# Low halves of the token mixers' projection weights by a negated copy and an adding transfer

## The chip, the cores and the metric

The kernel runs on one core of a Trainium2 chip. The metric is the device time of one execution in microseconds (us). The engines are named as in the profile: PE is TensorE (PEld its weight loads), ACT ScalarE, DVE VectorE, POOL GpSimd, SP SyncE; SP and POOL issue the transfers (DMAs). A time difference of about 0.2% (2.5 us) is what a measurement of this kernel can tell from no change.

## The reference

The trunk of an encoder with 512 tokens of width 1024, in float32, in two layers. Cut to what matters here:

```
x, mem                                  # 512 x 1024, 256 x 1024
layer A: h = rmsnorm(x)
  proj = h @ a_w_in                     # 1024 x 3336: q,k (conv, silu) | v | o | gates | q_mem
  mix  = mlstm(q, k, v, gates) * sigmoid(o)
  x += concat(mix, memory_attention(q_mem, mem)) @ a_w_out
  x += conv_ffn(rmsnorm(x))             # ffn_w_up 1024 x 5632, ffn_w_down 2816 x 1024
k, v = rmsnorm(x) @ w_kv                # 1024 x 1536, shared
layer B: h = rmsnorm(x)
  q, q_mem = h @ b_w_in                 # 1024 x 1024
  x += concat(band_attention(q, k, v), memory_attention(q_mem, mem)) @ b_w_out
  x += conv_ffn(rmsnorm(x))
return rmsnorm(x)
```

## The kernel before, in words

Every large product is made of three matmuls in the type float32r, which holds fewer bits than float32. A float32 operand a is written as two halves: the high one is a rounded to float32r, the low one is a minus the high one. The product is then high times high, high times low and low times high, added up in PSUM (`mm3`, L161 to L164; the low half of the weights is read in L164). Activations are split when they are made. Weights are split as they arrive: SP loads a tile of 128 x 1024 floats (512 KB) into one of three raw buffers `wr` (`load`, L135), ACT casts it to the high half `wh` (L129), and DVE subtracts that from the raw tile and writes the low half `wl` (L130); `parts` and `weights` (L147 to L155) are these two steps. `wh` and `wl` have three buffers each too, so a tile can be prepared once the tile three places earlier has been used up.

`project` (L166) takes eight row blocks of 128 of one column block of weights as a tile and makes 24 matmuls of 128x512 with it. It is called by `qk_tile` (12 tiles), `o_tile` (6) and `a_memory_queries` (2) on `a_w_in`, by `project_pair` (12 tiles of `w_kv`, 6 of `b_w_in`) and `b_memory_queries` (2) in layer B, and by `OutProjection.finish` and `ffn_hidden`, which take other weights. I number the twenty tiles of layer A that `project` loads as A1 to A20 and the twenty of layer B as B1 to B20, in the order in which they are used. A1 follows the value columns of `a_w_in` (`value_columns`, whose tiles have 384 columns and are split in the old way before and after the change); B1 follows the last eight tiles of layer A's `ffn_w_down`.

Projections are the filler between the steps of the mixers: `weave` (L193) takes so many steps of the filler for each step of the attention job. The program is written with a tile framework whose scheduler sets the order on each engine from costs of its own, save for what is pinned, so a change in one place can move instructions elsewhere. Each engine then works its own list strictly in order. POOL's list holds transfers (`xspill` L898 and L956, `rep` L932 and L934, the bias rows of the band attention L1004) and small memsets (L480 for the query heads, L631 for the convolution).

Of the kernel before, what the change touches and what calls it, by code (L numbers as in the profile page):

```python
# [10 lines left out]
F32R = mybir.dt.float32r  # L11
I32 = mybir.dt.int32
AF = mybir.ActivationFunctionType
ALU = mybir.AluOpType
AX = mybir.AxisListType

P = 128
D = 1024
# [9 lines left out]
DFF = 2816  # L28
# [13 lines left out]
def f(ap):  # L42
    return ap.bitcast(F32)
# [3 lines left out]
def trunk(  # L47
# [19 lines left out]
    V, A, G = nc.vector, nc.scalar, nc.gpsimd  # L67
# [10 lines left out]
    def sb(tag, shape, dtype=F32):  # L78
        count[0] += 1
        return pool.tile(shape, dtype, tag=tag, name=f"{tag}{count[0]}", bufs=bufs[tag])  # L80

    def ps(tag):
        count[0] += 1
        return psum.tile([P, S], F32, tag=tag, name=f"p{tag}{count[0]}", bufs=pbufs[tag])
# [43 lines left out]
    def split(hi, lo, src, on_act=True, pinned=False):  # L128
        high = A.copy(hi, src) if on_act else V.tensor_copy(hi, src)  # L129
        low = V.tensor_tensor(out=lo, in0=src, in1=f(hi), op=ALU.subtract)  # L130
        if pinned:
            pin(high)
            pin(low)

    def load(src, a, b, extra=None):  # L135
        n = b + (extra.shape[-1] if extra is not None else 0)
        raw = sb("wr", [P, D])[:, : a * n].rearrange("p (a b) -> p a b", a=a)
        if isinstance(src, list):
            for i, one in enumerate(src):
                nc.sync.dma_start(raw[:, i, :], one)  # L140
        else:
            nc.sync.dma_start(raw[:, :, :b], src)
        if extra is not None:
            nc.sync.dma_start(raw[:, :, b:], extra)
        return raw

    def parts(raw, pinned=False):  # L147
        _, a, b = raw.shape
        hi = sb("wh", [P, D], F32R)[:, : a * b].rearrange("p (a b) -> p a b", a=a)
        lo = sb("wl", [P, D], F32R)[:, : a * b].rearrange("p (a b) -> p a b", a=a)  # L150
        split(hi, lo, raw, pinned=pinned)
        return hi, lo

    def weights(*args):
        return parts(load(*args))  # L155

    def rows(w, c0, n, k0=0, k1=None):
        k1 = k1 if k1 is not None else w.shape[0] // P
        return w[k0 * P : k1 * P, c0 : c0 + n].rearrange("(k p) c -> p k c", p=P)

    def mm3(o, lh, ll, rh, rl, first, last):  # L161
        nc.tensor.matmul(o, lh, rh, start=first, stop=False)  # L162
        nc.tensor.matmul(o, lh, rl, start=False, stop=False)  # L163
        nc.tensor.matmul(o, ll, rh, start=False, stop=last)  # L164

    def project(w, c0, act, tag="mm"):  # L166


        n = len(act)
        wh, wl = weights(rows(w, c0, P), n, P)  # L170
        o = ps(tag)
        for k in range(n):
            mm3(o, wh[:, k, :], wl[:, k, :], act[k][0], act[k][1], k == 0, k == n - 1)
            yield
        return o

    def run(gen):
        while True:
            try:
                next(gen)  # L180
            except StopIteration as end:
                return end.value
# [5 lines left out]
    def pair_of(a, b):  # L188
        first = yield from a
        second = yield from b  # L190
        return first, second

    def weave(job, filler, each, lead=0):  # L193

        due = lead
        for n in chain([0], job):
            due += each if n is None else each * n
            while due >= 1:
                due -= 1
                next(filler, None)  # L200
# [39 lines left out]
    class Norm:  # L240
# [14 lines left out]
        def finish(self):  # L255

            yield 5.4
            o = ps("sc")
            for T in range(TT):
                tc.keep_in_program_order(  # L260
                    nc.tensor.matmul(
                        o[:, T : T + 1], self.acc[:, T * P : (T + 1) * P], ones[:, 0:1], start=True, stop=True
                    )
                )
            self.factor(o[:, :TT])
            yield 8.4
            self.spread()
# [19 lines left out]
    def scaled(t, g):  # L287
        hi, lo = sb("u", [P, S], F32R), sb("u", [P, S], F32R)
        A.activation(hi, t, AF.Copy, scale=g)
        V.scalar_tensor_tensor(lo, t, g, f(hi), op0=ALU.mult, op1=ALU.subtract)  # L290
        return hi, lo
# [117 lines left out]
    with tc.manual_schedule(engines={mybir.EngineType.PE, mybir.EngineType.Activation, mybir.EngineType.DVE}):  # L409

        w = ps("mm")
# [7 lines left out]
        for q in range(KT // 2 + 1):  # L419
            if q < KT // 2:  # L420
# [6 lines left out]
                hi, lo = sb("u", [P, S], F32R), sb("u", [P, S], F32R)  # L427
# [160 lines left out]
    class OutProjection:  # L588
# [19 lines left out]
        def finish(self, gnames):  # L608
            norm = Norm()
            acts = [[] for _ in gnames]  # L610
            for j in range(KT):
                o = self.o[j] if j in self.o else run(project(self.w, j * P, self.mixes))
                V.tensor_add(xT[j], xT[j], o)
                norm.add(xT[j])
                for a, g in zip(acts, gnames):
                    a.append(scaled(xT[j], g[:, j : j + 1]))
            return norm, acts

    def ffn_hidden(l, j, act, norm):
        w = ffn_w_up[l]  # L620
        fw, fb = col[f"fw{l}"], col[f"fb{l}"]
        gate, up = project(w, DFF + j * P, act), project(w, j * P, act, "sc")
        og = ou = None
        if norm.row is None:
            both = pair_of(gate, up)
            weave(norm.finish(), both, 1)
            og, ou = run(both)
        else:
            og = run(gate)
        pre = sb("t", [P, S + 4])  # L630
        G.memset(pre[:, 0:2], 0.0)  # L631
        V.tensor_tensor(out=pre[:, 2 : S + 2], in0=og, in1=norm.row, op=ALU.mult)  # L632
        acc = sb("t", [P, S])
        A.activation(acc, pre[:, 0:S], AF.Identity, scale=fw[:, j : j + 1], bias=fb[:, j : j + 1])  # L634
        for c in (1, 2):
            V.scalar_tensor_tensor(  # L636
                acc, pre[:, c : c + S], fw[:, c * FT + j : c * FT + j + 1], acc, op0=ALU.mult, op1=ALU.add
            )
        A.activation(acc, acc, AF.Silu)  # L639
        V.tensor_mul(acc, acc, norm.row)  # L640
        if ou is None:
            ou = run(up)
        hid = sb("t", [P, S])
        V.tensor_tensor(out=hid, in0=ou, in1=acc, op=ALU.mult)
        hi, lo = sb("u", [P, S], F32R), sb("u", [P, S], F32R)
        split(hi, lo, hid)
        return hi, lo
# [6 lines left out]
    act = acts  # L654
# [282 lines left out]
    for ci, (j0, j1) in enumerate(CHUNKS):  # L937
# [6 lines left out]
        if last:  # L944
            norm2, kvact, act = Norm(), [], []
        for j in range(KT):
            wh, wl = weights(rows(ffn_w_down[0], j * P, P, j0, j1), j1 - j0, P)
            o = ps("mm")
# [174 lines left out]
    for ci, (j0, j1) in enumerate(CHUNKS):  # L1123
        hid = []
        for j in range(j0, j1):
            hid.append(ffn_hidden(1, j, act, norm))
            if ci == 0:
                token_major(j % TT, j // TT)
        last = ci == len(CHUNKS) - 1
        n = (j1 - j0) // 2  # L1130
        for hf in range(2):
# [6 lines left out]
            for Ts, pieces in groups:  # L1138
                for c in pieces:
                    if c.start:  # L1140
                        os_[Ts[0]] = ps("mm")
                    for u in range(n):
                        if ws[u] is None:
                            ws[u] = weights(rows(ffn_w_down[1], hf * S, S, j0 + 2 * u, j0 + 2 * u + 2), 2, S)
                        wh, wl = ws[u]
# [59 lines left out]
```

## Time and profile before

| | |
|---|---|
| median of three runs | 1232.52 us (1232.07 to 1232.56) |
| the profiled execution's own time | 1232.33 us |
| its span, first to last instruction | 1230.5 us |
| granted TensorE clock | 0.999 |
| PE busy | 1219.2 us (99%) |
| DVE, ACT, POOL busy | 807.4, 560.5, 55.3 us |
| mean DMA rate | 106 GB/s |

The profile is that of one execution. A share of busy time is an average over stages; the table of windows gives it by stage. The chain that ended last is followed back from the last instruction, each step to what released it. A row of a timeline gives start, duration, engine, line, operation, and tiles as out<-in, with the idle time before it and its releaser in brackets. Layer A's projections A1 to A20 lie between 73 us and 222 us of the span, layer B's between 642 us and 796 us.

### The profile page before, as it was taken

The numbers are of one execution on the slowest core, as the hardware profiler recorded it, in microseconds if no ns is written. First come the engines' busy times: TensorE is split into PE (matmuls) and PEld (weight loads), VectorE is DVE, ScalarE is ACT, GpSimd is POOL, SyncE is SP. The second block draws the span as 40 slices with busy tenths as digits, with TensorE's granted clock in tenths as the row PEclk, the third lists the DMA queues.
The fourth block names the chain that finished last, engine by engine and source line by source line (L and its number), as shares of the span: only waits on it lengthen the run. The fifth ranks groups of instructions, "written<-read, shape, count | busy, mean of one in ns | idle before, by whom it ended". The sixth has DMA issues, their size and how long they took to land.

```text
span 1230.5 us, 15552 instructions
## 1 busy us (share of the span) xinstructions
PE 1219.2 (99%) x5839; PEld 1022.7 (83%) x5839; DVE 807.4 (66%) x1427; ACT 560.5 (46%) x911; POOL 55.3 (4%) x155
## 2 busy tenths in 40 slices
PE   9999999999999999999999999999999999999997
PEld 8988888888888888888888888888888888888886
DVE  7877687787564466445688888987656255544555
ACT  4546576644332233223365677775334123322334
POOL 1300000000000011000011000000000000000000
PEclk9999999999999999999999999999999999999999
DMA  8634111333344344424263323243232333323321
GB/s 271 210 90 120 53 53 56 116 103 104 103 113 110 104 126 129 125 87 113 77 180 113 93 70 98 61 141 112 88 102 86 103 90 99 103 87 101 103 86 69
DMA packets 190301, 130.63 MB, mean 106 GB/s; under 512 B 6328, under 2 KB 177810, under 8 KB 190226
## 3 DMA queue, kind: packets, MB, share of 16 engines
q1 hardware_dynamic: 186130, 116.59, 31.7%
q0 software_dynamic: 4096, 13.05, 3.8%
q8 instruction: 46, 0.75, 0.3%
q14 instruction: 29, 0.24, 0.1%
HBM read 122.08 MB, written 11.47 MB: 109 GB/s over the span
## 4 chain that ended last, share of the span: by engine, by line
PE 95%; ACT 2%; DVE 1%; DMA 0%; issue 0%; SPq 0%; DVEq 0%; ACTq 0%
PE pmm L162 20%; PE pmm L163 19%; PE pmm L164 19%; PE psc L162 8%; PE psc L163 8%; PE psc L164 8%; PE psc L500 2%; PE ptr L164 1%; PE ptr L162 1%; PE ptr L163 1%; PE ptr L1029 1%; PE ptr L1050 1%; PE ptr L1051 1%; DMA u<-in_mem_dram 0%; PE ptr L569 0%; PE ptr L583 0%
## 5 line engine op out<-in xcount | busy, mean ns | idle before, releaser
L129 ACT CAST wh<-wr 128x1024 fp32r<-128x1024 f32 (+2 forms) x208 | 210.1, 1012 | 432.9 <-issue 178.1
L162 PE MATMUL pmm<-u,wh 128*128 128x512 f32 (+1 forms) x960 | 378.0, 394 | 0.0
L164 PE MATMUL pmm<-u,wl 128*128 128x512 f32 (+1 forms) x960 | 373.9, 390 | 0.0
L163 PE MATMUL pmm<-u,wh 128*128 128x512 f32 (+1 forms) x960 | 373.6, 389 | 0.1
L130 DVE TENSOR_TENSOR wl<-wr,wh 128x1024 fp32r<-128x1024 f32 (+2 forms) x208 | 243.9, 1173 | 98.3 <-ACT wh L129 97.7
L164 PEld LDWEIGHTS pmm<-u,wl 128*128 128x128 f32 x960 | 180.4, 188 | 36.6
L163 PEld LDWEIGHTS pmm<-u,wh 128*128 128x128 f32 x960 | 180.7, 188 | 33.1 <-DVE u L130 0.5
L162 PEld LDWEIGHTS pmm<-u,wh 128*128 128x128 f32 x960 | 180.6, 188 | 32.8
L162 PE MATMUL psc<-u,wh 128*128 128x512 f32 x368 | 143.6, 390 | 0.0
L164 PE MATMUL psc<-u,wl 128*128 128x512 f32 x368 | 143.3, 389 | 0.0
L163 PE MATMUL psc<-u,wh 128*128 128x512 f32 x368 | 143.2, 389 | 0.0
L632 DVE TENSOR_TENSOR t<-pmm,rb 128x512 f32<-128x512 f32 x44 | 30.5, 692 | 116.1 <-PE pmm L164 116.0
L163 PEld LDWEIGHTS psc<-u,wh 128*128 128x128 f32 x368 | 69.1, 188 | 14.2
L162 PEld LDWEIGHTS psc<-u,wh 128*128 128x128 f32 x368 | 69.1, 188 | 14.3
L164 PEld LDWEIGHTS psc<-u,wl 128*128 128x128 f32 x368 | 69.1, 188 | 14.2
L636 DVE SCALAR_TENSOR_TENSOR t<-t,cols,t 128x512 f32<-128x512 f32 x88 | 65.9, 749 | 3.4 <-ACT t L634 1.9
L639 ACT ACTIVATE t<-t 128x512 f32<-128x512 f32 x44 | 27.8, 632 | 83.3 <-DVE t L636 83.3
L951 DVE TENSOR_TENSOR u<-u,pmm 128x512 f32<-128x512 f32 x24 | 16.5, 688 | 56.8 <-PE pmm L164 56.7
L640 DVE TENSOR_TENSOR t<-t,rb 128x512 f32<-128x512 f32 x44 | 30.5, 693 | 29.8 <-ACT t L639 29.8
L162 PE MATMUL pmm<-wh,u 128*128 128x512 f32 (+3 forms) x128 | 45.8, 363 | 1.5 <-ACT wh L129 1.5
L163 PE MATMUL pmm<-wl,u 128*128 128x512 f32 (+3 forms) x128 | 46.0, 360 | 0.0
L164 PE MATMUL pmm<-wh,u 128*128 128x512 f32 (+3 forms) x128 | 45.5, 358 | 0.0
(261 smaller groups left out, 1609.0 us busy)
## 6 DMA issues: line engine op xcount, KB each, us to landing
wr<-in_ffn_w_up_dram SPq DMA_DIRECT2D x88, 512.0 KB, 3.8
wr<-in_ffn_w_down_dram SPq DMA_DIRECT2D x38, 512.0 KB, 3.7
wr<-in_a_w_in_dram SPq DMA_DIRECT2D x20, 512.0 KB, 3.7
wr<-in_w_kv_dram SPq DMA_DIRECT2D x12, 512.0 KB, 3.8
xspill<-u POOLq DMA_DIRECT2D x16, 256.0 KB, 2.6
u<-xspill SPq DMA_DIRECT2D x16, 256.0 KB, 4.8
wr<-in_b_w_in_dram SPq DMA_DIRECT2D x8, 512.0 KB, 4.2
rep<-in_b_rel_row_dram POOLq DMA_DIRECT2D x12, 320.0 KB, 4.7
```

The source lines that it names most:

```text
L129: high = A.copy(hi, src) if on_act else V.tensor_copy(hi, src)
L130: low = V.tensor_tensor(out=lo, in0=src, in1=f(hi), op=ALU.subtract)
L162: nc.tensor.matmul(o, lh, rh, start=first, stop=False)
L163: nc.tensor.matmul(o, lh, rl, start=False, stop=False)
L164: nc.tensor.matmul(o, ll, rh, start=False, stop=last)
L500: nc.tensor.matmul(o, a, b, start=first and i == 0, stop=i == 1)
L632: V.tensor_tensor(out=pre[:, 2 : S + 2], in0=og, in1=norm.row, op=ALU.mult)
L636: V.scalar_tensor_tensor(acc, pre[:, c : c + S], fw[:, c * FT + j : c * FT + j + 1], acc, op0=ALU.mult, op1=ALU.add)
L639: A.activation(acc, acc, AF.Silu)
L640: V.tensor_mul(acc, acc, norm.row)
L951: V.tensor_add(xT[j], xT[j], o)
L1029: nc.tensor.transpose(tp[:, b * P : (b + 1) * P], es[T, h][:, b * P : (b + 1) * P], ident)
```

## The change

`project` gets another way to make its halves, `summed_weights`, as default; the calls in `OutProjection.finish` and `ffn_hidden` keep the old one. In the new way ACT casts the raw tile to `wh` as before, then writes minus `wh` into `wl`, and POOL issues a transfer that reads the same weights from DRAM once more and adds them to `wl`. So 40 tiles lose the DVE subtraction and get a second ACT instruction and a POOL transfer of 512 KB (1024 rows of 512 bytes); 168 other tiles stay as they were. The raw buffer `wr` is now free after the cast.

```diff
+    def summed_weights(src, a, b):
+        raw = load(src, a, b)
+        hi = sb("wh", [P, D], F32R)[:, : a * b].rearrange("p (a b) -> p a b", a=a)
+        lo = sb("wl", [P, D], F32R)[:, : a * b].rearrange("p (a b) -> p a b", a=a)
+        A.copy(hi, raw)
+        A.activation(lo, f(hi), AF.Copy, scale=-1.0)
+        G.dma_start(lo, src, accum_op=ALU.add)
+        return hi, lo
...
-    def project(w, c0, act, tag="mm"):
+    def project(w, c0, act, tag="mm", halves=summed_weights):
...
-        wh, wl = weights(rows(w, c0, P), n, P)
+        wh, wl = halves(rows(w, c0, P), n, P)
...
-                o = self.o[j] if j in self.o else run(project(self.w, j * P, self.mixes))
+                o = self.o[j] if j in self.o else run(project(self.w, j * P, self.mixes, "mm", weights))
...
-        gate, up = project(w, DFF + j * P, act), project(w, j * P, act, "sc")
+        gate, up = project(w, DFF + j * P, act, "mm", weights), project(w, j * P, act, "sc", weights)
```

In the changed file the new function takes ten lines, so what stood at L167 or below stands ten lines lower; its own lines are L162 (the cast), L163 (the negation) and L164 (the transfer).

The first place is ACT in layer A, where the casts of A3, A4 and A5 stood as follows before (`wh_1086`, `wh_1138`, `wh_1187`; `pmm_993` is the result of A1, L784 and L788 are the convolution's first term and the silu).

```order
L129 CAST wh_1086<-wr_1084 128x1024
L129 CAST wh_1138<-wr_1136 128x1024
L784 ACTIVATE t_1021<-pmm_993,cols_539 128x512
L788 ACT_TABLE_LOAD
L788 ACTIVATE t_1021<-t_1021 128x512
L784 ACTIVATE t_1074<-pmm_1037,cols_539 128x512
L129 CAST u_1027<-t_1021 128x512
L129 CAST wh_1187<-wr_1185 128x1024
```

The same place on ACT after the change (A3, A4 and A5 are `wh_1088`, `wh_1141` and `wh_1191`; L784 and L788 are now L794 and L798).

```order
L162 CAST wh_1088<-wr_1086 128x1024
L163 ACTIVATE wl_1089<-wh_1088 128x1024
L162 CAST wh_1141<-wr_1139 128x1024
L794 ACTIVATE t_1022<-pmm_994,cols_539 128x512
L163 ACTIVATE wl_1142<-wh_1141 128x1024
L798 ACT_TABLE_LOAD
L798 ACTIVATE t_1022<-t_1022 128x512
L162 CAST wh_1191<-wr_1189 128x1024
L129 CAST u_1028<-t_1022 128x512
L163 ACTIVATE wl_1192<-wh_1191 128x1024
```

Each cast is followed by its negation, for A4 and A5 with one other instruction between the two, and the second L784 has moved behind A5.

The second place is POOL at the start of layer B, before: the last spills of x, the memsets of the first query heads, the first bias rows.

```order
L956 DMA xspill<-u_2362 128x512
L956 DMA xspill<-u_2364 128x512
L956 DMA xspill<-u_2366 128x512
L480 MEMSET u_5674 64x512
L480 MEMSET u_5675 64x512
L1004 DMA bias_5708<-rep_3927 128x512
L1004 DMA bias_5710<-rep_4007 128x512
```

And POOL there after the change (`wl_5546`, `wl_5606`, `wl_5664` and `wl_5710` belong to B1 to B4; L956 is now L966, L1004 is L1014, L480 is L490).

```order
L966 DMA xspill<-u_2382 128x512
L164 DMA wl_5546<-in_w_kv_dram 128x8x128
L966 DMA xspill<-u_2384 128x512
L164 DMA wl_5606<-in_w_kv_dram 128x8x128
L966 DMA xspill<-u_2386 128x512
L164 DMA wl_5664<-in_b_w_in_dram 128x8x128
L164 DMA wl_5710<-in_w_kv_dram 128x8x128
L1014 DMA bias_5732<-rep_3947 128x512
L1014 DMA bias_5734<-rep_4027 128x512
L490 MEMSET u_5697 64x512
```

The adding transfers stand between the spills, and the bias rows and the memsets stand behind the transfer of B4.

The third place is ACT around A17 to A19, where the second pair of memory-attention casts (`pt`) stands, before (A18 and A19 are `wh_2143` and `wh_2224`; L788 is a silu, L519 and L490 lead to the third mLSTM head's keys).

```order
L129 CAST pt_1807<-ptr_1965 128x2x256
L129 CAST pt_1808<-ptr_1978 128x2x256
L129 CAST wh_2143<-wr_2141 128x1024
L129 CAST wh_2224<-wr_2222 128x1024
L519 COPY t_2008<-ptr_1988 64x512
L788 ACTIVATE t_1943<-t_1943 128x512
L519 COPY t_2008<-ptr_1999 64x512
L490 CAST u_1949<-t_1943 64x512
L490 CAST u_1950<-t_1943 64x512
```

The same place after the change (A17 and A18 are `wl_2076` and `wh_2160`; L788, L519 and L490 are now L798, L529 and L500).

```order
L129 CAST pt_1820<-ptr_1980 128x2x256
L163 ACTIVATE wl_2076<-wh_2075 128x1024
L129 CAST pt_1821<-ptr_1993 128x2x256
L162 CAST wh_2160<-wr_2158 128x1024
L529 COPY t_2023<-ptr_2003 64x512
L163 ACTIVATE wl_2161<-wh_2160 128x1024
L798 ACT_TABLE_LOAD
L798 ACTIVATE t_1957<-t_1957 128x512
L529 COPY t_2023<-ptr_2014 64x512
L500 CAST u_1963<-t_1957 64x512
L500 CAST u_1964<-t_1957 64x512
```

Ahead of the key casts stand two negations and a table load more, and the cast of A19 has moved behind them.

## The prediction

> **What bounds the kernel now.** I read the page first, then PE's waits, then the windows.
>
> ```profile
> PE 1219.2 (99%) x5839; PEld 1022.7 (83%) x5839; DVE 807.4 (66%) x1427; ACT 560.5 (46%) x911; POOL 55.3 (4%) x155
> ...
> PE 95%; ACT 2%; DVE 1%; DMA 0%; issue 0%; SPq 0%; DVEq 0%; ACTq 0%
> ```
>
> PE is busy for 99% of the span and carries 95% of the chain that ended last. The waits of PE (for whom, us in total, times, longest) tell how little is left to win:
>
> ```profile
> PE pmm L162 <- ACT wh L129: 1.5, 1, 1.5
> ...
> PE ptr L569 <- DVE t L560: 0.3, 1, 0.3
> PE pmm L164 <- DVE u L130: 0.2, 1, 0.2
> PE psc L500 <- ACT t L557: 0.2, 1, 0.2
> PE ptr L1029 <- DVE pt L130: 0.2, 1, 0.2
> ```
>
> The 1.5 us is one wait for a value tile, ahead of A1. Nowhere does PE wait for `wl` of L130. So the change can give PE at most a few tenths of a microsecond; what it can do is make PE wait. The question is whether the new `wl` comes in time.
>
> **How much time a tile has.** A tile's buffers come free with the last matmul of the tile three places earlier, so there is room for about two tiles' matmuls between the cast and the need. The need is the start of the first L164 matmul that reads `wl`. These are the needs of A1 to A7 and B1, from PE's timeline, and among them the last L163 of A3 (90.11), which frees A6's buffer:
>
> ```profile
> 73.98 0.40 PE L164 MATMUL pmm<-u,wl 128*128 128x512 f32 x1
> 79.45 0.39 PE L164 MATMUL pmm<-u,wl 128*128 128x512 f32 x1
> 84.89 0.39 PE L164 MATMUL pmm<-u,wl 128*128 128x512 f32 x1
> 90.11 0.39 PE L163 MATMUL pmm<-u,wh 128*128 128x512 f32 x1
> 90.33 0.39 PE L164 MATMUL pmm<-u,wl 128*128 128x512 f32 x1
> 95.77 0.39 PE L164 MATMUL pmm<-u,wl 128*128 128x512 f32 x1
> 102.02 0.40 PE L164 MATMUL pmm<-u,wl 128*128 128x512 f32 x1
> 107.82 0.40 PE L164 MATMUL pmm<-u,wl 128*128 128x512 f32 x1
> 642.96 0.39 PE L164 MATMUL pmm<-u,wl 128*128 128x512 f32 x1
> ```
>
> And these are ACT's rows: the casts of A1 to A4, the silu ahead of A5's cast, the cast of A7, then B1's cast with the two instructions behind it.
>
> ```profile
> 65.74 1.06 ACT L129 CAST wh<-wr 128x1024 fp32r<-128x1024 f32 x1 [4.53 <-PE psc L164]
> 69.60 1.05 ACT L129 CAST wh<-wr 128x1024 fp32r<-128x1024 f32 x1 [2.80 <-PE psc L164]
> 74.09 1.05 ACT L129 CAST wh<-wr 128x1024 fp32r<-128x1024 f32 x1
> 78.97 1.05 ACT L129 CAST wh<-wr 128x1024 fp32r<-128x1024 f32 x1 [3.83 <-PE pmm L163]
> 85.04 0.63 ACT L788 ACTIVATE t<-t 128x512 f32<-128x512 f32 x1
> 99.10 1.04 ACT L129 CAST wh<-wr 128x1024 fp32r<-128x1024 f32 x1
> 634.36 1.05 ACT L129 CAST wh<-wr 128x1024 fp32r<-128x1024 f32 x1 [1.31 <-issue]
> 635.32 0.63 ACT L252 ACTIVATE t<-u 128x512 f32<-128x512 f32 x1
> 635.85 1.32 ACT L289 ACTIVATE u<-u,cols 128x512 fp32r<-128x512 f32 x2
> ```
>
> The casts of A1, A2 and A4 start when PE lets the buffer go, so they can't come earlier.
>
> **The change part by part.** *The negation.* No row shows a copy of 128x1024 from SBUF with a factor on ACT. The nearest are the cast of that size, 1.05 us, and the scaling L289 of half the size, 1.32 us for two; both say 1.05 to 1.3, and I take 1.05. Forty of them are 42 us more for ACT, which is busy for 560.5; they count only where ACT is late already.
>
> The room that is left for the transfer is need minus the end of the negation. A1: 65.74 + 1.06 + 1.05 = 67.9, so 73.98 − 67.9 = 6.1 us. A2: 69.60 + 2.10 = 71.7, so 7.8. A3: 74.09 + 2.10 = 76.2, so 8.7. A4 has L794 (0.78 by the row of L784 below) between cast and negation: 78.97 + 1.05 + 0.78 + 1.05 = 81.9, so 8.4. A5's cast stands behind the silu: 85.67 + 1.05, then the cast `u` (0.6) and the negation give 88.4, so 7.4. A6's cast now stands ahead of a silu and starts when its buffer is free, at 90.5: with the cast, L794, the silu (0.63) and the negation 94.0, so 8.0. A7: 99.10 + 2.1 = 101.2, so 6.6. B1 has L252 and the first half of L289 between the two in the new order: 635.85 + 0.66 + 1.05 = 637.6, so 5.4. From A8 on and from B2 on projections share PE with the mixers, and the room is mostly 10 us or more.
>
> *The transfer.* The trace has no adding transfer. Call D its time from the issue on POOL to landing. The nearest rows (KB each, median us from issue to landing):
>
> ```profile
> wr<-in_a_w_in_dram SPq DMA_DIRECT2D x20, 512.0 KB, 3.7
> ...
> bias<-rep POOLq DMA_DIRECT2D x12, 256.0 KB, 3.4
> ```
>
> The same weights plainly from SP take 3.7 us: the lower end. For the rest I need the pure transfer time, from the windows (length; busy and count of PE, PEld, DVE, ACT, POOL; clock, DMA share, GB/s):
>
> ```profile
> 74.00:108.00 34.00, 34.00 (x156) 27.98 (x155) 27.01 (x48) 20.42 (x29) 0.00 (x0) 1.00 0.36 103
> ...
> 630.00:643.00 13.00, 13.00 (x59) 10.74 (x59) 11.55 (x16) 8.79 (x13) 1.62 (x3) 1.00 0.63 190
> ```
>
> In the first, 0.36 × 34 = 12.2 us of all 16 DMA engines moved 103 GB/s × 34 us = 3.5 MB, so 512 KB take 1.8 us. From POOL a 256 KB load takes 3.4, of which 0.9 is transfer, so 2.5 is fixed, and a plain 512 KB would take 4.3. Adding must also read what lies in `wl`: estimated as a second pass of 1.8, that is 6.1. And each transfer meets a plain load: `wr` comes free at the cast's end, SP then issues the load for three tiles later, and the adding transfer starts 1 us behind it; sharing the engines costs up to another 1.8, so 7.9. Last, POOL must describe 1024 rows instead of 128:
>
> ```profile
> L1004 POOL DMA_DIRECT2D bias<-rep x12 | 6.8, 568 | 96.9 <-DVE s L1014 95.8 <-DVE s L1019 0.9
> ...
> L934 POOL DMA_DIRECT2D rep<-maskf x12 | 6.6, 548 | 53.2 <-DMA rep<-in_b_rel_row_dram 53.2
> ```
>
> 128 rows cost POOL 0.57 us and the 64 rows of L934 cost 0.55: rows seem nearly free, but eight times 0.55 is 4.4. So D lies between 3.7 and 7.9 + 3.9 = 11.8; I take 8.0, next to the sum without dear rows.
>
> [...]
>
> *The sum at D = 8.0.* A1 is late by 8.0 − 6.1 = 1.9 us. That shifts the needs behind it, so A2 (7.8) and A3 (8.7) are in time; A4 (8.4) and A6 (8.0) are too, though their buffers shift along. A5: 0.6. A7: 1.4. B1: 2.6. Together 6.5 us.
>
> *ACT's own chain.* At one place ACT holds up PE today without a margin:
>
> ```profile
> 185.40 0.96 ACT pt L129 x2
> 186.38 2.00 ACT wh L129 x2
> ...
> 190.81 0.70 DVE u L491
> 191.55 0.74 PE psc L500 x2
> ```
>
> In the chain of waits ACT runs without a break from 178.8 to 190.8, then DVE, then PE's L500. The new order puts two negations (2.1) and a table load (1.28 by the row of L788 below) in there and takes one cast (1.0) out: 2.4 us later at most, nothing if PE, whose own list moved too, has other matmuls to do. I take 1.2, the middle, since no row decides.
>
> ```profile
> L784 ACT ACTIVATE t<-pmm,cols 128x512 f32<-128x512 f32 x12 | 9.3, 775 | 0.0
> ...
> L788 ACT ACT_TABLE_LOAD x6 | 7.7, 1283 | 9.6 <-DVE t L787 6.3 <-DVE s L881 3.2
> ```
>
> *What costs nothing.* DVE loses 40 of the 208 subtractions, some 47 us at the page's mean of 1.17; it is off PE's path, so this gives nothing. POOL, 55 us busy, gets 40 issues of 0.55 or more; what is queued behind them are memsets and bias rows. The first bias rows now stand behind B4's transfer, whose cast starts at 648.90:
>
> ```profile
> 648.90 1.05 ACT L129 CAST wh<-wr 128x1024 fp32r<-128x1024 f32 x1 [3.57 <-issue]
> ...
> L1014 DVE CUSTOM_DVE_ANT_0 t<-psc,bias x48: 276/482/692, 664.5 to 826.6; 128x128 f32<-128x128 f32 x12, 128x256 f32<-128x256 f32 x12, 128x384 f32<-128x384 f32 x12, 128x512 f32<-128x512 f32 x12
> ```
>
> They are issued by 652 and land by 657, at the slowest 5 us of today, and L1014 reads them at 664.5. Should B4's negation be late by more than 7 us, the band attention waits for the rest.
>
> [...]
>
> So 6.5 + 1.2 = 7.7 us on the profiled execution's 1232.33 (0.19 under the median, 1.8 over its span): **1240.0 us**.
>
> **The rivals.** *In time after all (not slower).* If the second pass overlaps with the first and the load has gone by, D is 6.1 or less: only B1 is late, by 0.7, and with no loss on ACT's chain the time is 1233.0. It decides at D = 6.8, where the sum passes 2.5 us (A1 0.7, A7 0.2, B1 1.4, with some of ACT's). For it: POOL's rows look free, and DMA engines are idle for two thirds of 74 to 108 us. Against it: B1 falls into the window with a DMA share of 0.63, and D would have to stay 1.2 us under my sum of passes. Chance 0.28.
>
> *DVE's relief shortens the kernel.* For it: DVE is busy for 27.0 of 34 us in A1 to A7. Against it: PE's waits for DVE from 45 us on are 0.7 us in the rows above. It gives 1231.6, and over 0.2% faster would be below 1230.0, for which no row has the room. Chance of that 0.05, for what a new order may do that I can't see.
>
> *POOL or the DMA engines can't keep up.* If rows are dear, D is 11.8: A1 5.7, A4 3.4, A5 11.8 − 7.4 − 3.4 = 1.0, A7 11.8 − 6.6 − 1.0 = 4.2, B1 6.4, ACT's chain 2.4: 23.1 us, 1255.4. Against it stands the nearly equal price of 64 and 128 rows. Chance 0.17.
>
> **How the numbers follow.** My forecast, slower by 3 to 15 us (D from 7 to 10), has 0.50 and the dear rows 0.17: slower 0.67. The measurement can tell 0.2%, 2.5 us. Same 0.28, faster 0.05. The range takes in the case in time (from 1232.0, no loss at all) and the dear rows with 4 us for later tiles: 1232.0 to 1260.0.
>
> **What would show it.** Right: a row of POOL's L164 transfers with about 8 us to landing; PE waits for `DMA wl` once at A1, at A5, A7 and B1, of 1 to 3 us each, and none at A2 and A3; PE's busy time unchanged. Wrong: a landing time of 6 us or less and no wait for `wl`; a wait of PE at each of the 40 tiles (then the transfers run at a rate of their own); or a longer POOL row (then rows are dear); or waits of PE on ACT outside 170 to 195 us.

## The result, and the profile after

| | before | after |
|---|---|---|
| median | 1232.31 us (1232.07 to 1232.56) | 1251.51 us (1250.51 to 1251.59) |
| ratio after to before | | 1.0154, 95% interval 1.0136 to 1.0172 |
| the profiled execution, its span | 1232.33, 1230.5 us | 1250.51, 1248.7 us |
| granted TensorE clock | 0.999 | 0.995 |

The change makes the kernel 19.2 us slower (1.5%). The forecast was 7.7 us slower: the sign is right and the time lies in the range, but more than half of the loss came from places for which the prediction had no term, or one that was too small. The 19.2 us lie outside the 3 to 15 us of the forecast proper; that the range holds them is luck, since its upper end was set by dear rows on POOL, which did not come true.

The page of the changed kernel: the engines' busy time, and the DMA issues (KB each, median us from issue to landing).

```profile
PE 1226.3 (98%) x5839; PEld 1023.7 (82%) x5839; DVE 765.7 (61%) x1387; ACT 601.0 (48%) x953; POOL 118.3 (9%) x195
...
wl<-in_a_w_in_dram POOLq DMA_DIRECT2D x20, 512.0 KB, 6.3
wl<-in_w_kv_dram POOLq DMA_DIRECT2D x12, 512.0 KB, 6.4
```

PE has the same 5839 matmuls and is busy for 7 us more; ACT gained 40 us, DVE lost 42 and POOL gained 63. In the median the adding transfer lands 6.3 us after its issue, not 8.0. By that alone nearly every tile should have been in time. The waits of PE tell another story (for whom, us in total, times, longest):

```profile
PE pmm L174 <- DMA wl<-in_a_w_in_dram: 6.1, 3, 4.8
PE pmm L174 <- DMA wl<-in_w_kv_dram: 2.7, 2, 1.9
PE pmm L172 <- ACT wh L129: 1.4, 1, 1.4
PE psc L510 <- DVE u L501: 1.1, 1, 1.1
```

Before, no wait for `wl` from DRAM could exist, and the longest were the one for `wh` (1.4 now, 1.5 then) and one of 1.1 for DVE's `mcf`, which both kernels have. Of the 8.8 us of waits for `wl` 4.8 are a single one. (The last row is one wait at 203 us for L501, L491 before, the step of DVE in which the prediction's chain of ACT ended.) Where the wait of 4.8 us lies is seen by following one tile, A16, through ACT, POOL and PE. ACT's timeline (start, duration, then the instruction; left out are exponentials with their accumulator reads, two casts and one L794, all without a pause):

```profile
168.36 1.05 ACT L162 CAST wh<-wr 128x1024 fp32r<-128x1024 f32 x1 [2.31 <-PE pmm L173]
169.42 1.28 ACT L567 ACT_TABLE_LOAD   x1
...
171.30 1.28 ACT L798 ACT_TABLE_LOAD   x1
172.60 0.63 ACT L798 ACTIVATE t<-t 128x512 f32<-128x512 f32 x1
173.25 1.28 ACT L567 ACT_TABLE_LOAD   x1
...
178.47 1.08 ACT L163 ACTIVATE wl<-wh 128x1024 fp32r<-128x1024 f32 x1
```

POOL's timeline there, and PE's:

```profile
179.91 1.54 POOL L164 DMA_DIRECT2D wl<-in_a_w_in_dram  x1 [12.71 <-ACT wl L163]
```

```profile
183.06 0.40 PE L173 MATMUL psc<-u,u 128*128 128x512 f32 x1
188.24 0.79 PE L174 MATMUL pmm<-u,wl 128*128 128x512 f32 x1 [4.79 <-DMA wl<-in_a_w_in_dram]
188.84 0.63 PE L172 MATMUL pmm<-u,wh 128*128 128x512 f32 x1
189.26 0.63 PE L173 MATMUL pmm<-u,wh 128*128 128x512 f32 x1
```

A16's cast ends at 169.4 and its negation could start at once. It starts 9 us later, because the new order of ACT puts thirteen instructions between the two, three loads of the activation table among them (the short reads of the accumulator behind the exponentials are not counted; the expectations below say twelve). The transfer then takes until 188.2, and PE, which ran dry at 183.5, stands for 4.8 us. (POOL had waited for this negation for 12.7 us: the transfer itself was ready.)

The rows behind the wait show a second loss. The matmuls come 0.43 us apart instead of some 0.23. The windows (length; busy and count of PE, PEld, DVE, ACT, POOL; granted clock, DMA share, GB/s) give the reason:

```profile
184.00:188.00 4.00, 0.00 (x0) 0.00 (x0) 1.54 (x3) 3.92 (x10) 0.00 (x0) 0.69 1.23 178
188.00:192.00 4.00, 3.76 (x9) 2.98 (x10) 2.53 (x6) 1.91 (x3) 1.54 (x1) 0.50 0.00 0
192.00:196.00 4.00, 4.00 (x21) 3.24 (x20) 0.00 (x0) 0.28 (x1) 0.00 (x0) 0.96 1.09 131
...
652.00:656.00 4.00, 2.24 (x10) 1.50 (x8) 2.62 (x4) 3.78 (x6) 2.12 (x2) 1.00 1.32 230
656.00:660.00 4.00, 3.83 (x10) 3.04 (x11) 1.36 (x2) 1.48 (x3) 1.56 (x1) 0.57 1.32 228
```

After the pause the granted clock is 0.50 for 4 us, in which PE does nine matmuls instead of some 18: 9 x 0.2 = 1.8 us more. The profile counts this as busy time of PE, so it stands in no list of waits. The same happens at 656 us, after B1's wait. The two stretches together are 3.6 of the 7 us by which PE is busier; the rest is not accounted for here.

The whole loss can be split by place: for each tile, the end of its last matmul in the timeline of PE, after less before. In us:

| | before | after | later by | grown by |
|---|---|---|---|---|
| A1 | 79.2 | 79.8 | 0.6 | 0.7 (it was 0.1 early) |
| A15 | 180.2 | 181.7 | 1.5 | 0.9 |
| A16 | 188.1 | 195.9 | 7.8 | 6.3 |
| A20 | 221.5 | 232.6 | 11.1 | 3.3 |
| last tile ahead of B1 | 642.7 | 653.8 | 11.1 | 0.0 |
| B1 | 649.1 | 664.0 | 14.9 | 3.8 |
| B17 | 771.4 | 788.2 | 16.8 | 1.9 |
| span's end | 1230.5 | 1248.7 | 18.2 | 1.4 |

### The profile page after: what moved, and what is told of

It is laid out like the page before. It is cut to its first block, busy times and chain, and to the rows that moved or that the text cites. A ratio compares the mean times of both kernels' runs of the same rounds, so it can differ in the third digit from the quotient of the medians.

```text
span 1248.7 us, 15620 instructions
## 1 busy us (share of the span) xinstructions
PE 1226.3 (98%) x5839; PEld 1023.7 (82%) x5839; DVE 765.7 (61%) x1387; ACT 601.0 (48%) x953; POOL 118.3 (9%) x195
## 4 chain that ended last, share of the span: by engine, by line
PE 89%; issue 3%; ACT 3%; DMA 3%; DVE 2%; POOL 0%; SPq 0%; POOLq 0%; DVEq 0%; ACTq 0%
PE pmm L172 18%; PE pmm L174 18%; PE pmm L173 18%; PE psc L172 8%; PE psc L174 8%; PE psc L173 8%; PE psc L510 2%; PE ptr L172 1%; PE ptr L174 1%; PE ptr L173 1%; PE ptr L1039 1%; DMA wl<-in_w_kv_dram 1%; DMA wl<-in_a_w_in_dram 1%; PE ptr L1060 1%; PE ptr L1061 1%
## 5 line engine op out<-in xcount | busy, mean ns | idle before, releaser
L129 ACT CAST wh<-wr 128x1024 fp32r<-128x1024 f32 (+3 forms) x168 | 168.2, 1002 | 396.1 <-issue 173.1
L130 DVE TENSOR_TENSOR wl<-wr,wh 128x1024 fp32r<-128x1024 f32 (+3 forms) x168 | 195.1, 1162 | 90.8 <-ACT wh L129 90.4
L641 POOL MEMSET t<- 128x2 f32 x44 | 4.4, 101 | 627.2 <-DVE t L654 491.4
L162 ACT CAST wh<-wr 128x1024 fp32r<-128x1024 f32 x40 | 41.9, 1050 | 34.4 <-PE pmm L173 26.9
L172 PE MATMUL pmm<-wh,u 128*128 128x512 f32 (+3 forms) x128 | 45.9, 364 | 1.4 <-ACT wh L129 1.4
```

The costliest lines, as they stand in the source:

```text
L162: A.copy(hi, raw)
```

## The experiments

The theory from this profile: most of the loss is not the transfer's time but ACT's list. It holds A16's negation far behind its cast, and it is so full around A17 to A19 that 40 us of negations and two more table loads delay what PE waits for there. The transfer itself costs only at A1 and B1, where the room is 6 us. The rivals: that the adding transfers cost by their length everywhere, or by POOL's and the DMA engines' load.

All times are medians in us; the kernel before ran beside them at 1232.35 to 1232.38. The last columns give where the profiled execution's delay grew, as in the table above.

| kernel | time | ratio, 95% interval | A1 | A2-15 | A16 | A17-20 | B1 | B2-17 | rest |
|---|---|---|---|---|---|---|---|---|---|
| the change | 1251.51 | 1.0136 to 1.0172 | 0.7 | 0.9 | 6.3 | 3.3 | 3.8 | 1.9 | 1.4 |
| negation early on ACT | 1243.69 | 1.0078 to 1.0108 | 1.1 | 0.8 | -1.6 | 5.0 | 0.8 | 3.9 | 0.8 |
| negation on DVE | 1238.92 | 1.0036 to 1.0069 | 0.6 | 4.8 | -0.6 | 0.6 | 1.6 | 0.2 | 0.1 |
| no transfer, DVE adds | 1240.44 | 1.0050 to 1.0080 | 0.0 | 1.0 | -1.0 | 4.6 | 0.0 | 2.4 | 0.1 |
| A16, A17 the old way | 1244.52 | 1.0082 to 1.0112 | 0.8 | 0.8 | 0.4 | -0.5 | 6.6 | 1.8 | 1.4 |
| layer A only | 1244.31 | 1.0080 to 1.0114 | 0.8 | 1.0 | 6.4 | 3.3 | 0.0 | -0.3 | 0.0 |
| layer B only | 1240.90 | 1.0051 to 1.0081 | 0.0 | 0.1 | 0.0 | -0.2 | 4.8 | 2.0 | 1.7 |
| DVE, roomy tiles only | 1234.26 | 1.0006 to 1.0025 | 0.0 | 1.6 | -0.6 | 0.5 | 0.0 | 0.1 | 0.2 |
| ACT early, roomy tiles only | 1242.17 | 1.0063 to 1.0093 | 0.0 | 1.8 | -1.6 | 4.9 | 0.0 | 3.2 | 1.2 |
| overwrite, not add | 1239.68 | 1.0040 to 1.0073 | 0.0 | 0.8 | 0.5 | 4.3 | 0.7 | 1.5 | 0.6 |
| negation on POOL | 1252.65 | 1.0154 to 1.0190 | 5.6 | 4.9 | 0.5 | -0.6 | 5.5 | 1.2 | 3.0 |

(What a profiled execution lost or won ahead of A1, up to 2.5 us in one of them, is left out of the columns.)

**Negation early on ACT.**

```diff
-        A.activation(lo, f(hi), AF.Copy, scale=-1.0)
+        with tc.high_priority():
+            A.activation(lo, f(hi), AF.Copy, scale=-1.0)
```

> The changed kernel, with one difference: the negation gets a higher priority with the scheduler, so that on ACT it stands one to three places behind its cast (one to twelve before, twelve for A16 and A17). The 40 transfers, the 40 negations and the two more table loads stay. Theory Q (the time is lost because a few negations stand far behind their cast in ACT's list, so PE waits there, and PE's clock falls after the longer waits): the wait of 4.8 us at A16 and the slow 4 us behind it go, A1 keeps its 0.5, B1 its 2 to 4; 1236 to 1240 us, and PE's wait for wl of a_w_in under 1.5 us. Rival R (the transfers' own time and traffic delay PE): no difference, 1249 to 1253. Rival L (ACT has too much to do with 40 negations and two table loads): 1247 to 1252.

The gap at A16 is gone and 7.8 us come back; the time, 1243.69, is above what the theory gave. PE's waits of this kernel (its lines stand one further down):

```profile
PE psc L173 <- ACT t L845: 1.0, 1, 1.0
PE pmm L175 <- DMA wl<-in_a_w_in_dram: 0.8, 1, 0.8
PE psc L511 <- ACT u L495: 0.8, 4, 0.2
PE ptr L594 <- DVE pt L130: 0.8, 1, 0.8
```

For `wl` only A1's 0.8 and B1's 0.5 are left, but 5.0 us at A17 to A20 and 3.9 in layer B remain, with waits on ACT and on DVE's work behind ACT. So the theory's "list" has two parts: one negation in a bad place, and a list that is too long.

**Negation on DVE.**

```diff
-        A.activation(lo, f(hi), AF.Copy, scale=-1.0)
+        V.tensor_scalar(lo, f(hi), -1.0, None, op0=ALU.mult)
```

> The changed kernel with the negation on DVE in place of ACT: ACT has its old load and its old 18 table loads, the 40 transfers stay. Theory Q: the negations now stand where the subtractions stood, which PE never waited for, so what is left is the transfer's 6.2 us against the room of A1 and B1; 1233 to 1240 us. Rival R (the transfers cost): 1248 to 1253. Rival L (ACT's load): 1232 to 1236, as far as the transfers cost nothing.

ACT's work is that of before, the transfers are all there, and the loss at A17 to A20 falls to 0.6. What is left are tiles that come late: DVE's list holds the negation of A4 and A5 until 85.6 and 93.1 us, where ACT had it ready at 82.3 and 88.4, and PE waits 1.7 and 1.6 us for them.

**No transfer.** ACT casts and negates as in the change, DVE adds the raw tile.

```diff
-        G.dma_start(lo, src, accum_op=ALU.add)
+        V.tensor_tensor(out=lo, in0=raw, in1=f(lo), op=ALU.add)
```

> The changed kernel with the transfer taken out: ACT casts and negates as in the change, and DVE adds the raw tile to the negated half. Same ACT load and 20 table loads, no POOL transfers. Theory Q: the tile has 5 us more room without the transfer; a negation far behind its cast can still cost a microsecond or two; 1232 to 1238 us. Rival R: 1232 to 1234, like the kernel before. Rival L: 1245 or more.

Without a single adding transfer the kernel loses 8.1 us, 4.6 of them at A17 to A20. It fell between the expectations: the load of ACT alone costs more than the theory then had for it. The windows of 170 to 205 us and 640 to 800 us, columns as above, first of the kernel before:

```profile
170.00:205.00 35.00, 34.93 (x174) 29.11 (x173) 27.53 (x50) 30.97 (x56) 1.04 (x2) 1.00 0.20 59
640.00:800.00 160.00, 159.84 (x813) 133.05 (x812) 137.79 (x336) 107.80 (x237) 14.81 (x28) 1.00 0.30 91
```

without the transfer (ACT negates),

```profile
170.00:205.00 35.00, 32.49 (x155) 25.76 (x153) 25.35 (x47) 34.59 (x59) 0.00 (x0) 1.00 0.16 42
640.00:800.00 160.00, 158.80 (x800) 130.73 (x799) 134.68 (x323) 124.23 (x248) 15.34 (x29) 1.00 0.31 91
```

and with the negation on DVE and all transfers.

```profile
170.00:205.00 35.00, 34.90 (x170) 28.63 (x169) 27.81 (x53) 31.16 (x55) 7.26 (x7) 1.00 0.82 131
640.00:800.00 160.00, 158.31 (x801) 131.57 (x800) 126.10 (x323) 105.62 (x228) 48.56 (x49) 1.00 0.83 158
```

The reader compares ACT and PE in the first rows. Before, ACT was busy for 31.0 of these 35 us, so it had 4 us to spare; here it is busy for 34.6, full, and PE falls to 32.5 us and 155 matmuls from 174. With the negation on DVE ACT is at 31.2 and PE at 34.9, though the DMA engines' share rises from 0.20 to 0.82. In this stretch ACT's list delays PE, not the transfers.

It isn't the negations alone that fill this list. Every kernel here in which ACT negates A17 has 20 table loads instead of 18, and the two more, 2.6 us together, both stand between 180 and 205 us. These are the kernels that lose 3.3 us or more at A17 to A20; those with 18 loads lose 0.6 or less there. The runs don't tell apart what the negations cost in this stretch and what the table loads do.

**Traffic alone, first try.** The kernel before, in which POOL also copies the weights of the forty tiles to a spare place in DRAM.

```diff
+        spare = dram.tile([P, D], F32, name=f"spare{c0}_{count[0]}").rearrange("p (a b) -> p a b", a=n)
         wh, wl = weights(rows(w, c0, P), n, P)
+        G.dma_start(spare, rows(w, c0, P))
```

> The kernel before with 40 transfers more on POOL: each projection tile of both mixers is also read once more from DRAM, plainly, and written to a spare place in DRAM that nobody reads; wl comes from DVE as before. So 512 KB of traffic per tile and POOL's longer list, and nothing waits for them. Theory Q and rival L: 1232 to 1234 us. Rival R, as far as traffic is the cost: 1237 or more.

1275.81 us, ratio 1.0331 to 1.0365. It doesn't test what it was meant to: the copies depend on nothing, the scheduler moved all forty into the first 98 us, eighteen of them into the first 40, and there they held up the first loads (weight loads issued in the first 45 us took up to 24 us to land, against 11.5 before). The first 45 us of this kernel and of the one before, in windows as above:

```profile
0.00:45.00 45.00, 32.27 (x206) 30.12 (x206) 23.32 (x61) 11.54 (x17) 19.41 (x31) 0.89 0.98 337
```

```profile
0.00:45.00 45.00, 41.37 (x298) 39.28 (x299) 37.34 (x88) 21.21 (x33) 9.25 (x30) 1.00 0.74 241
```

At 337 GB/s PE gets only 206 matmuls done there, not 298. Of the 43 us in the span 42.6 are lost by A1's end.

**A16 and A17 in the old way.**

```diff
-        o = yield from project(w_in, c * P, act)
+        o = yield from project(w_in, c * P, act, "mm", weights if c == 5 else summed_weights)
...
-        o = yield from project(w_in, 3 * AW + j * P, act)
+        o = yield from project(w_in, 3 * AW + j * P, act, "mm", weights if j == 4 else summed_weights)
```

> All of the change, except that A16 and A17 (the two tiles whose negation stands 12 instructions behind their cast on ACT) are split in the old way; ACT has 18 table loads again instead of 20. Theory of the list (the scheduler's place for the negation costs, not the transfer): the gap of 4.8 us at A16 goes, and with it the slow matmuls behind it (6.3 us together at A16's end), part of the 3.2 us at A17 to A19 goes with the table loads; the rest (A1 0.6, B1 3.9, layer B 3) stays: 1241 to 1245 us, 6 to 10 under the changed kernel. Rival, that the transfers' number and traffic cost: 38 of 40 stay, so 1250 to 1251.

Two tiles out of forty give back 7.0 us, and the whole 9.6 of A16 to A20: with them the two extra table loads go. The negations of A18 to A20 are still on ACT, and PE doesn't wait for them in the stretch that was full:

```profile
170.00:205.00 35.00, 35.00 (x170) 28.64 (x169) 25.69 (x49) 33.72 (x58) 3.35 (x3) 1.00 0.47 89
```

So three negations on ACT without the table loads fit into these 35 us. B1 lost 2.8 us more than in the change; its transfer took 8.7 us instead of 7.2. How long it takes there differs from kernel to kernel, between 6.4 and 8.7 us. Loads, spills of x and the next adding transfer are under way beside it (DMA share 1.32 in the window of 652 to 656 us above); whether one of these decides, and which, no run shows.

**Layer A only, and layer B only.** `project` gets `weights` in the other layer's calls, for layer A only:

```diff
-        ov = yield from project(w_kv, AW + j * P, kvact)
+        ov = yield from project(w_kv, AW + j * P, kvact, "mm", weights)
```

and so on for the three other calls of layer B; for layer B only, the same in the three of layer A.

> The new way in layer A only (A1 to A20). By the delays of the changed kernel tile by tile, layer A carries 11 of its 18 us (A16 6.3, A17 to A19 3.2, A1 0.6, 1 elsewhere): 1242 to 1245 us, a wait of some 5 us at A16 as the only long one, and no delay that grows behind 225 us. Rival, that each transfer costs by its traffic alike: half of 19, 1241 to 1242, spread over the twenty tiles.

> The new way in layer B only (B1 to B20). By the delays tile by tile layer B carries 7 us (B1 3.9, the gap of 1.9 us and slow matmuls behind it; 2.2 at B18; some 1 of drift): 1238 to 1241 us, with one wait of about 2 us at B1. Together with the kernel that has only layer A the excess over the kernel before should add up to the 19 us of the whole change within 2; if it adds up to much less, the two layers share a cause.

11.9 and 8.5 us: together 20.4 against the 19.2 of both. The layers' losses are separate. Behind layer A nothing grows, and each layer shows its long wait:

```profile
PE pmm L174 <- DMA wl<-in_a_w_in_dram: 6.4, 3, 4.9
```

```profile
PE pmm L174 <- DMA wl<-in_w_kv_dram: 4.2, 2, 3.0
```

**Traffic alone, second try.** The kernel before, in which POOL sends each finished `wl` from SBUF to a spare place in DRAM, so that the transfer can't come early.

```diff
+            G.dma_start(spare.rearrange("p (a b) -> p a b", a=n), f(wl))
```

> The kernel before, in which POOL also sends each finished low half wl of the forty tiles from SBUF to a spare place in DRAM that nothing reads: 40 transfers of 512 KB with 1024 rows at the times and from the engine of the adding transfers, with no one waiting for them but the reuse of the buffer three tiles later. Theory that the traffic itself costs nothing: 1232 to 1234 us. Rival, that POOL's descriptors and the traffic slow other transfers or PE's operand reads: 2 us or more, spread over the tiles, 1235 to 1240.

1235.0, ratio 1.0012 to 1.0031. Most of the 2.1 us in its span is one wait of 1.7 us for an exponential of ACT at 114 us; behind that nothing grows. ACT's order is that of before there, but its casts of two weight tiles wait 2.0 and 2.2 us for their plain loads, which took 4.5 and 7.2 us to land, against 3.7 and 3.8 before. The second of the two casts, before and here:

```profile
106.98 1.05 ACT L129 CAST wh<-wr 128x1024 fp32r<-128x1024 f32 x1 [0.44 <-PE pmm L163]
```

```profile
109.74 1.05 ACT L129 CAST wh<-wr 128x1024 fp32r<-128x1024 f32 x1 [2.24 <-DMA wr<-in_a_w_in_dram]
```

A transfer to the spare place was issued 0.3 us behind the load of 7.2 us. So the rival's mechanism, traffic that slows other transfers, is seen at one place, and the time lies at the rival's lower end. The transfer was not what was meant, though: the spare tile lies row by row, so it took POOL 0.54 us and 128 rows, not 1024. It says only that 20 MB more of traffic at these places cost some 2 to 3 us in all.

**Roomy tiles only, negation on DVE.** A1 to A6, B1 and B2 in the old way; 32 adding transfers are left.

```diff
+        V.tensor_scalar(lo, f(hi), -1.0, None, op0=ALU.mult)
...
+        o = yield from project(w_in, c * P, act, "mm", weights if c in (0, 6, 1, 7) else summed_weights)
...
+        o = yield from project(w_in, 3 * AW + j * P, act, "mm", weights if j < 2 else summed_weights)
...
+        ov = yield from project(w_kv, AW + j * P, kvact, "mm", weights if j == 0 else summed_weights)
...
+        o = yield from project(w_kv, j * P, kvact, "mm", weights if j == 0 else summed_weights)
```

> Negation on DVE instead of ACT, and A1 to A6, B1 and B2, the tiles with the least room, split in the old way; 32 tiles keep the negated copy and the adding transfer. Theory that the loss is only lateness at the tight tiles and ACT's list: the waits for wl that cost the kernel with the negation on DVE 6.2 us (A1 0.7, A4 2.0, A5 1.9, B1 1.6) go, 1232 to 1235 us. [...]

1234.26, 1.9 us over the kernel before. Thirty-two adding transfers with their POOL rows are in, and PE's one wait for them is 0.4 us:

```profile
PE pmm L174 <- DMA wl<-in_a_w_in_dram: 0.4, 1, 0.4
```

So all 32 of them, with the negations on DVE, cost no more than these 1.9 us where there is room. Did every adding transfer cost alike wherever it stands, four fifths of the 6.6 us that the kernel with the negation on DVE and all forty loses would have stayed, a time of some 1237.6. It is the fastest of the versions that were run, and it doesn't beat the kernel before.

**The same tiles, negation early on ACT.**

```diff
-        V.tensor_scalar(lo, f(hi), -1.0, None, op0=ALU.mult)
+        with tc.high_priority():
+            A.activation(lo, f(hi), AF.Copy, scale=-1.0)
```

> Negation on ACT with high priority (it stands one or two instructions behind its cast), and A1 to A6, B1 and B2 split in the old way. No tile is late by then. Theory that the negations load ACT's list where PE waits for it (A17 to A19 and layer B): about 5 us at A17 to A19 and 2 to 3 in layer B stay, 1238 to 1242 us, though no wait of PE for wl is over 0.5 us. Rival, that only lateness of wl costs: 1232 to 1235.

1242.17, just above the range of the theory: the negation's engine, and on ACT its priority with the scheduler, are the only differences in the code, and they are worth 7.9 us. PE waits for `wl` nowhere for longer than 0.1 us; the window of 170 to 205 us, first of the kernel with the negation on DVE and then of this one, shows the full ACT again.

```profile
170.00:205.00 35.00, 35.00 (x173) 28.82 (x172) 25.96 (x51) 31.76 (x57) 9.64 (x9) 1.00 0.76 125
170.00:205.00 35.00, 32.75 (x154) 25.57 (x153) 20.03 (x41) 34.69 (x59) 7.16 (x6) 1.00 0.70 113
```

**Overwrite instead of add.** The product is another one here, since `wl` holds the full weights. The order on ACT is that of the change.

```diff
-        G.dma_start(lo, src, accum_op=ALU.add)
+        G.dma_start(lo, src)
```

> The whole change, but the transfer overwrites wl with the weights instead of adding to it (wl is then the full weights, so the product is another one); the lists of all engines are those of the changed kernel. It measures what the adding itself costs a transfer: by the prediction's second pass 1.8 us, landing 4.3 to 5.0 us after the issue instead of 6.4, the gap at A16 falls from 4.8 to 3.0 to 3.6, the one at B1 under 1.5 with no slow matmuls behind it: 1244 to 1248 us. Rival, that POOL's 1.5 us for 1024 rows and not the second pass makes the transfer long: landing after 6 us or more, 1249 to 1251.

From the page and the groups of POOL in this kernel:

```profile
wl<-in_a_w_in_dram POOLq DMA_DIRECT2D x20, 512.0 KB, 4.5
```

```profile
L164 POOL DMA_DIRECT2D wl<-in_a_w_in_dram x20 | 17.6, 879 | 143.6 <-ACT wl L163 106.0 <-PE psc L510 14.7 <-PE psc L885 9.6
```

and POOL's group in the changed kernel:

```profile
L164 POOL DMA_DIRECT2D wl<-in_a_w_in_dram x20 | 30.8, 1538 | 135.7 <-ACT wl L163 108.7 <-PE psc L510 11.9 <-PE psc L885 8.7
```

The adding makes a transfer 1.8 us longer (6.3 against 4.5). The landing is as the estimate of a second pass has it, but not all of the 1.8 need be a second pass: POOL's row got shorter too (1.54 to 0.88), and these 0.66 us may be part of it. The run doesn't tell the two apart. The time, 1239.68, is below both expectations: the gap at A16 shrank from 4.8 to 1.0, not to 3.0, since A16's transfer took 8.3 us with adding and 4.6 without, and the slow matmuls behind it went too. But A17's negation is as badly placed, and a wait of 2.0 us turned up there, with slow matmuls behind it.

**Negation on POOL.**

```diff
-        A.activation(lo, f(hi), AF.Copy, scale=-1.0)
+        G.tensor_scalar(lo, f(hi), -1.0, None, op0=ALU.mult)
```

> The whole change, with the negation on POOL, ahead of the transfer in the same list, so that neither ACT nor DVE has it. No trace of this case shows a copy with a factor on POOL; the nearest rows are its memsets of 64x512, 0.5 us, which would make 1 to 2 us for 128x1024. Theory of lateness: ACT's list is that of the kernel with the negation on DVE, the waits for wl are as there or up to 1 us longer at A1, A4, A5 and B1: 1238 to 1243 us. Rival, that POOL becomes the bound (negation over 4 us): over 1250.

1252.65: the rival's time, but not by its mechanism. From POOL's groups:

```profile
L163 POOL TENSOR_SCALAR wl<-wh 128x1024 fp32r<-128x1024 f32 x40 | 115.3, 2882 | 104.9 <-ACT wh L162 104.7
```

2.88 us, above the 1 to 2 and under the 4 that would make POOL the bound. A1 and B1 are then late by 3.7 and 3.5 us and lose 5.6 and 5.5; behind both waits the granted clock is lower, as in these windows of 2 us:

```profile
78.12:80.12 2.00, 2.00 (x5) 1.61 (x6) 1.99 (x5) 0.00 (x0) 1.70 (x2) 0.59 1.33 242
80.12:82.12 2.00, 2.00 (x7) 1.57 (x6) 0.09 (x1) 0.00 (x0) 1.22 (x1) 0.56 1.21 156
...
657.31:659.31 2.00, 2.00 (x8) 1.60 (x9) 2.00 (x2) 0.26 (x1) 2.00 (x2) 0.86 1.24 268
659.31:661.31 2.00, 2.00 (x6) 1.61 (x5) 1.14 (x2) 0.00 (x0) 1.70 (x2) 0.50 1.46 199
```

At A16 to A20, with ACT free, nothing is lost: it agrees on ACT, and shows what 2 us more ahead of the transfer cost at the tight tiles.

## Why the prediction was wrong

**Right.** PE is the bound and the change can only make it wait. A1's and B1's lateness: the room at A1 was put at 6.1 us; PE was ready at 74.0 and the negation ended at 67.8, 6.2. At B1 it was put at 5.4, and was 5.6 (648.6 to 654.2). The waits there were forecast as 1.9 and 2.6 and came out as 0.5 and 1.9. The negation's 1.05 us is 1.06. DVE's relief of 42 us shows in no shorter time. Adding costs the 1.8 us at which the second pass was estimated, though POOL's longer row may be up to 0.66 of them, so the fit is in part luck: the transfer lands after 6.3 us where it adds and after 4.5 where it overwrites. The second pass itself was the author's estimate, and no run shows it.

**D.** Taken as 8.0; it was 6.3 in the median, 8.1 to 8.3 at A2, A3 and A16, and 7.2 to 10.5 at B1 to B3, where three such transfers overlap. The sum had put 1.8 us on every transfer for the plain load that it meets; the median is near the sum without that, 6.1. At A2 and A3 the sum with it fits: the plain load issued beside them at 75.1 us took 6.6 us, against 3.7 before, and A2's transfer landed just as PE came to it (80.06 and 80.10 us). With 6.3 A5 and A7 are in time, as they were, and of the 6.5 us only 1.1 are left (A1 0.2, B1 0.9). So this term was too large by 5 us, which the next ones hid.

**The step that failed: "From A8 on and from B2 on projections share PE with the mixers, and the room is mostly 10 us or more."** The room was reckoned from a negation right behind its cast. For A1 to A7 and B1 I had taken the instructions between the two from the new order; behind that I had not. A16 needed `wl` at 183.5 and its cast ended at 169.4: with the negation in between, 13 us of room for a transfer that took 6.5 to 8.3 us there. Thirteen instructions of ACT, three of them table loads of 1.28 us, took 9 of these. This one tile cost 6.3 of the 18.2 us, and the run with A16 and A17 in the old way and the one with the negation early both took it back. B18, whose negation stands nine instructions behind its cast, has a wait of 0.75 us.

**ACT's own chain: 1.2, measured 3.3.** The prediction saw that ACT runs without a break from 178.8 to 190.8 and that two negations and a table load would go in, 2.4 us at most, and halved it. Of the 3.3 us that the change lost at A17 to A20, 1.1 are PE's wait for L501, behind ACT, and 0.8 a wait for A19's transfer. The pair of kernels that differ in the negation's engine and priority shows 4.4 us between them at A17 to A20 (4.9 against 0.5; 3.4 if A16's column is added), with ACT at 34.7 of 35 us. The high bound of 2.4 counted what is put in between 178.8 and 190.8 us alone; but in the whole stretch of 170 to 205 us ACT had only 4 us to spare, and three negations and two table loads make 5.7. How much of the loss is the one and how much the other stays open. In layer B behind B1, of which the prediction said nothing, the same pair shows 4.1 more (4.4 against 0.3), with one table load there in both. At A17 to A20 the change itself lost less than the kernel with the early negation, 3.3 against 5.0. Its ACT stands idle for 5.8 us after A17's negation, until PE has got going again:

```profile
195.72 0.59 ACT L129 CAST pt<-ptr 128x512 fp32r<-128x512 f32 x1 [5.81 <-PE ptr L579]
```

That it caught up during A16's wait, and so lost less, is argued, not shown.

**The clock.** No term had it. The pause of 4.8 us and the one of 1.9 cost some 1.8 us each again in slow matmuls.

**POOL.** "Costs nothing" held as far as PE's waits show, none of which is for POOL's other work, but not for the reason given: POOL's row for a transfer of 1024 rows took 1.54 us, not 0.55. That was the rival of the dear rows, at a chance of 0.17; they cost 1 us per transfer, far from the 3.9 of that case. POOL's transfers in the changed kernel (duration in ns, shortest, median and longest; first and last start):

```profile
L164 POOL DMA_DIRECT2D wl<-in_a_w_in_dram x20: 1527/1530/1608, 68.1 to 216.4; - x20
L164 POOL DMA_DIRECT2D wl<-in_w_kv_dram x12: 1532/1582/1616, 648.9 to 782.5; - x12
L164 POOL DMA_DIRECT2D wl<-in_b_w_in_dram x8: 1536/1552/1593, 656.0 to 791.4; - x8
```

All forty last 1.53 to 1.62 us. Thirteen of them have a cast or tensor_scalar of DVE beside them, and these last 1.53 to 1.60. With the negation on DVE three of the forty rows are longer, up to 1.82 us at 93.4 us, each with a tensor_scalar of DVE beside it (the one at 93.8 us took 1.01 us itself, against 0.70 in the mean); with the roomy tiles only, three of 32 are, up to 2.19 us. What makes these few rows longer no run shows.

Of the signs that the prediction named as speaking against itself, one came true as it was worded: a POOL row longer than 0.55 us. Waits outside the places that it named came true too (A16, A19, B18, and none at A5 and A7), but as waits for `wl`, with ACT's lateness hidden behind the transfer.

What stays open: what makes B1's transfer take 6.4 us in one kernel and 8.7 in another, and so whether 0.8 or 6.6 us are lost there.

## What to carry to other kernels

When a step is split into two instructions on one engine with a transfer behind the second, count the instructions that the new order puts between the two for every tile, not for the tight ones only: a tile with 13 us of room lost 9 of them in another engine's queue. Ahead of adding work to an engine that is "46% busy", take its share in the stretch where the bound engine waits for it (31 of 35 us here), and count the table loads that the new order brings with the work itself. Adding transfers were nearly free where their tiles had room (32 of them cost 1.9 us in all), but relieving DVE, which was not the bound, won nothing; whether they pay where the relieved engine is the bound no run here shows.

## What the runs showed of the hardware

A pause of PE can cost more than its length: at A16 PE waited for 4.8 us and 6.3 were lost. No pause of 1.68 us or less was followed by a fall of the granted clock. Of the fifteen pauses of 1.94 us or more in these runs (the program's start and end left out), fourteen came with half the clock, for some 3 to 6 us from their end (8 in one, with a further pause in them). The windows show it, first after the pause of 1.68 us that ended at 92.9 us (negation on DVE):

```profile
93.00:97.00 4.00, 4.00 (x18) 3.31 (x19) 3.86 (x8) 1.49 (x3) 3.54 (x3) 1.00 0.73 165
```

and then in and after the one of 3.9 us that ended at 651.1 us (A16 and A17 in the old way):

```profile
648.00:651.00 3.00, 0.00 (x0) 0.00 (x0) 1.36 (x2) 2.46 (x4) 2.14 (x2) 0.74 1.36 235
651.00:655.00 4.00, 3.87 (x9) 3.11 (x10) 0.00 (x0) 0.00 (x0) 0.00 (x0) 0.50 1.32 201
```

The fifteenth, of 1.98 us, ended at 13.4 us in the first traffic run and left the clock at 1.00, while another of 1.98 us (overwrite, not add, at 194.4 us) halved it. What decides at this length no run shows; the fifteenth's window:

```profile
13.37:15.37 2.00, 2.00 (x16) 1.88 (x16) 0.69 (x1) 0.59 (x1) 0.00 (x0) 1.00 1.05 382
```

The same 128x1024 tile is negated in 1.06 us on ACT, 0.70 on DVE and 2.88 on POOL. POOL's row for a transfer of 1024 rows lasts 0.88 us where it is plain (overwrite, not add) and 1.54 where it adds, against 0.57 for 128 plain rows before.
